# Fixed places for the weight tiles of column products, and later transposes, in a one-core decoder layer

## Chip, core and metric

The kernel runs on one core of a Trainium2 chip. The metric is the device time of one launch in microseconds. The kernel before takes 2506.86 us in the median of three runs (2506.35 to 2507.48). All times below are microseconds unless marked ns. The engines go by the names of the profile: PE (TensorE, matmuls), PEld (its weight loads), DVE (VectorE), ACT (ScalarE), POOL (GpSimd), SP (SyncE, which here issues the DMAs).

## What is computed

One hybrid decoder layer in float32 on 256 tokens with 2048 features:

```python
h = rmsnorm(x, ffn1_norm_pre)
x = x + 0.5 * rmsnorm((silu(h @ w_gate) * (h @ w_up)) @ w_down, ffn1_norm_post)   # D_FF = 5632
h = rmsnorm(x, mix_norm_pre)
c_q, c_kv, k_rope, hq, hf, hi, hg, gate_a, gate_b = split_columns(h @ w_in)       # 512, 512, 64, 6 x 2048
y_a = mla_branch(...)     # 16 heads; latents normed, up-projected, rotary part of 64, causal softmax
y_b = hgrn2_branch(...)   # 16 heads; gated linear recurrence over chunks
y = (sigmoid(gate_a) * y_a + sigmoid(gate_b) * y_b) @ w_out
x = x + rmsnorm(y, mix_norm_post)
h = rmsnorm(x, ffn2_norm_pre)
x = x + 0.5 * rmsnorm((silu(h @ w_gate) * (h @ w_up)) @ w_down, ffn2_norm_post)
```

All products are float32 in accuracy. The kernel gets it by splitting every operand into a rounded part `hi` (type fp32r) and the rest `lo`, and by computing hi x hi + hi x lo + lo x hi.

## The kernel before

Tokens are two tiles of 128 (`tt` = 0, 1). An operand of a product lies in one tile of 128 partitions x 2 x 16 x 256 floats: `hi` and `lo` of 16 slices (k) of 128 features by 256 tokens, features on the partitions. Such operands are h1, after1 and h2 (one tag, so one address), oa and ob (one tag), mg, and, with four slices, cqT and ckvT. The trace names the first three h, after and h.

**Weights.** `load_w` (L89) fetches 512 KB (128 x 1024 floats, tile `raw`, four buffers) by a DMA from SP's queue. ACT casts it to `whi` (L106) and DVE subtracts to get `wlo` (L107). `whi` and `wlo` come from `part` (L85): four buffers each of 1088 floats a partition, of which 1024 are used from an offset `place` on, counted in floats. `places` gives one offset for `whi` and one for `wlo`.

**Column products** (`gemm_t`, L116) give features by tokens: the weights are the stationary operand (loaded into PE before each matmul), the operand's slices are streamed. A weight group of 1024 columns serves 4 slices x 2 output blocks. For each of these 8 there is a pair: `wlo` over the 256 tokens of the operand's `hi` (L133) and `whi` over the 512 columns of `hi` and `lo` (L134). In the first slice of a product the two stand in the other order (L130, L131). A product has `kt / 4` groups: four for 16 slices, one for cqT and ckvT. `round` (L110) hands out the places, a new combination for each group in the order of the program: group i has `whi` at i % 8 * 8 and `wlo` at i // 8 % 8 * 8 floats, a multiple of 32 bytes each.

**Row products** (`gemm_n`, L153) give tokens by features: the operand's slices are stationary and `whi`, `wlo` are streamed, three matmuls a slice and token tile (L149 to L151). Both parts lie at `place`, which is SAME = 32 floats unless told otherwise. With `late`, the second token tile's matmuls are held back and run after the first tile's; `hooks` are pairs of a position and a function. The position is a fraction: from -1 to 0 over the first half, from 0 to 1 over the held half.

The program has 528 column groups. In their order: 160 in the first FFN, 48 in the MLA part (gates of after, and cqT and ckvT), 32 of oa, 76 in the HGRN2 part (after), 52 of ob and the last gates, 160 in the second FFN.

**End of a block.** `closing` (L271) runs four row products. The last one holds its second half back (16 slices). At position 0, `end` (L289) finishes the norm of token tile 0 and updates x; at HOOK = 0.7, `begin` (L299) builds the next operand of tile 0: `prenorm` (L257) does for four quarters of 512 features a broadcast load, a DVE product into `xn` (two buffers), four PE transposes (L249 in `transposed`) and the split on ACT and DVE (L190, L191). Tile 1 follows inside the next product (`w_cq` of the mixer, `gate0` of the second FFN) by a hook at NEXT = -0.1. DVE's products and the splits are pulled ahead in the planner by a priority of 400.

**MLA.** `latent` (L543) norms a 512-wide latent: ACT square sum, POOL power, DVE scaling into `xn` (L552), then PE transposes and the split. It runs for c_q, then, after the product with `w_ckv`, for c_kv. The rotary key product (L578 to L587) and `gate(0)` follow, then its rotation and two transposes (L600). `q_rope` (L607) makes the rotary queries: a product, DVE and POOL rotation into `xn`, PE transposes (L614). `heads_in` (L618) makes two heads' operands with column products of cqT and ckvT; between them `step` takes one deferred function from `later`.

PE runs its instructions in one order, which a planner (a list by priority and estimated readiness) fixes when the program is built. It starts from the program's order and may let ready work pass.

Of the kernel before, what the change touches and what calls it, by code (L numbers as in the profile page):

```python
# [9 lines left out]
F32 = mybir.dt.float32  # L10
# [4 lines left out]
ALU = mybir.AluOpType  # L15
# [4 lines left out]
P = 128  # L20
T = 256
NT = 2
D = 2048
KD = D // P
# [4 lines left out]
KL = LORA // P  # L29
NH = 16  # L30
ROPE = 64
# [6 lines left out]


AHEAD = 400  # L40
HOOK = 0.7
NEXT = -0.1


WARM = 10
# [1 line left out]
SAME = 32  # L47
# [17 lines left out]
class Ops:  # L65


    def __init__(self, ctx, tc, a):
        self.tc, self.nc, self.a = tc, tc.nc, a
        self.const = ctx.enter_context(tc.tile_pool(name="const", bufs=1))  # L70
        self.wp = ctx.enter_context(tc.tile_pool(name="wp", bufs=1))
        self.small = ctx.enter_context(tc.tile_pool(name="small", bufs=3))
        self.hp = ctx.enter_context(tc.tile_pool(name="hp", bufs=1))
        self.mm = ctx.enter_context(tc.tile_pool(name="mm", bufs=2, space=PSUM))
        self.tp = ctx.enter_context(tc.tile_pool(name="tp", bufs=2, space=PSUM))
        self.sp = ctx.enter_context(tc.tile_pool(name="sp", bufs=2, space=PSUM))
        self.dram = ctx.enter_context(tc.tile_pool(name="dram", bufs=1, space=DRAM))
        self.slots = KF // 4
        self.count = 0
        self.mhalf = self.const.tile([P, 8], F32, name="mhalf")  # L80
        self.nc.vector.memset(self.mhalf, -0.5)
        self.ident = self.const.tile([P, P], F32, name="ident")
# [24 lines left out]
        nc.vector.tensor_tensor(out=lo, in0=raw, in1=hi.bitcast(F32), op=ALU.subtract)  # L107
        return hi, lo

    def round(self):  # L110

        i = self.count
        self.count += 1
        return i % 8 * 8, i // 8 % 8 * 8

    def gemm_t(self, w, act, kt, tick=None):  # L116

        nc = self.nc  # L120
        ps = self.mm.tile([P, 2, 512], F32, name="mm")
        for g in range(kt // 4):
            hi, lo = self.load_w(w[g], places=self.round())
            for i in range(4):
                k = g * 4 + i
                for j in range(2):
                    c = slice(i * 256 + j * P, i * 256 + (j + 1) * P)
                    both = act(k)
                    if k == 0:
                        nc.tensor.matmul(ps[:, j], hi[:, c], both, start=True, stop=False)  # L130
                        nc.tensor.matmul(ps[:, j, 0:T], lo[:, c], both[:, 0], start=False, stop=False)  # L131
                    else:
                        nc.tensor.matmul(ps[:, j, 0:T], lo[:, c], both[:, 0], start=False, stop=False)  # L133
                        nc.tensor.matmul(ps[:, j], hi[:, c], both, start=False, stop=k == kt - 1)  # L134
            if tick:
                tick()
        return ps
# [116 lines left out]
    def ahead(self):  # L254
        return self.tc.high_priority(AHEAD)

    def prenorm(self, x, wname, act, tt):  # L257

        for c in range(4):
            with self.ahead():  # L260
                w = self.bcast(wname, c)
                xn = self.small.tile([P, 512], F32, name="xn", bufs=2)
                self.nc.vector.tensor_tensor(out=xn, in0=x[:, c * 512:(c + 1) * 512], in1=w, op=ALU.mult)  # L263
            self.transposed(xn, act, c, tt)

    def weighted(self, ps, c, z, wname):

# [3 lines left out]
    def closing(self, w, act, kt, late, own, pool, post, half, x_src, x_dst, nxt):  # L271

        z = [pool.tile([P, D], F32, name="z", tag=f"z{tt}") for tt in range(NT)]
        yssq = [self.ssq4() for _ in range(NT)]
        for c in range(3):
            ps = self.gemm_n(w[c], act, kt)
            for tt in range(NT):
                self.square_sum(yssq[tt][:, c:c + 1], ps[:, tt], D, half)  # L280
                self.weighted(ps[:, tt], c, z[tt], post)
        rest = [self.small.tile([P, 1], F32, name="rest", bufs=4) for _ in range(NT)]
        for tt in range(NT):
            self.known(rest[tt], yssq[tt][:, 0:3], half)
        x = [pool.tile([P, D], F32, name="x", tag="s8", bufs=self.slots) for tt in range(NT)]
        for tt in range(NT):
            self.nc.sync.dma_start(out=x[tt], in_=x_src[tt])

        def end(ps, tt):  # L289
            self.square_sum(yssq[tt][:, 3:4], ps[tt], D, half)  # L290
            rstd = self.rstd(yssq[tt][:, 3:4], rest[tt])
            self.weighted(ps[tt], 3, z[tt], post)
            for c in range(4):
                cs = slice(c * 512, (c + 1) * 512)
                self.nc.vector.scalar_tensor_tensor(out=x[tt][:, cs], in0=z[tt][:, cs], scalar=rstd, in1=x[tt][:, cs],  # L295
                                                    op0=ALU.mult, op1=ALU.add)
                self.nc.sync.dma_start(out=x_dst[tt, :, cs], in_=x[tt][:, cs])

        def begin(tt):  # L299
            if nxt is None:  # L300
                return
            wname, act, fac = nxt
            self.prenorm(x[tt], wname, act, tt)
            ssq = self.ssq4()
            for c in range(4):
                self.square_sum(ssq[:, c:c + 1], x[tt][:, c * 512:(c + 1) * 512], D)
            self.factor(fac, ssq, tt)

        ps = self.gemm_n(w[3], act, kt, late=late, pool=pool, own=own,
                         hooks=[(0, lambda ps: end(ps, 0)), (HOOK, lambda _: begin(0))])  # L310
        end(ps, 1)
        return [(NEXT, lambda _: begin(1))]


@with_exitstack
# [223 lines left out]
def mla(ops, mp, c_q, hm, h, fac, rows, oa, gate):  # L539
    nc, a, small, tp, sp, ident = ops.nc, ops.a, ops.small, ops.tp, ops.sp, ops.ident  # L540
    V, S, G = nc.vector, nc.scalar, nc.gpsimd

    def latent(ps, name, norm):  # L543
        w = ops.bcast(norm, 0)
        res = mp.tile([P, 2, KL, T], F32R, name=name)
        for tt in range(NT):
            ssq = small.tile([P, 1], F32, name="cssq")
            y = ps[tt] if isinstance(ps, list) else ps[:, tt]
# [1 line left out]
            rstd = ops.rstd(ssq, fac[:, tt, 1:2])  # L550
            cn = small.tile([P, LORA], F32, name="xn", bufs=2)
            V.scalar_tensor_tensor(out=cn, in0=y, scalar=rstd, in1=w, op0=ALU.mult, op1=ALU.mult)  # L552
            ops.transposed(cn, res, 0, tt)
        return lambda k: res[:, :, k, :]

    def rope(dst, src, tt, n):

# [12 lines left out]
    cos, sin = rope_tables(ops, mp)  # L570
    amask = mp.tile([P, 3, P], F32, name="amask")
    nc.sync.dma_start(out=amask, in_=a["amask"])
    cq = latent(c_q, "cqT", "mla_q_norm")
    ckv = latent(ops.gemm_n(a["w_ckv"][0], h, KD), "ckvT", "mla_kv_norm")

    hi, lo = ops.load_w(a["w_krope"][0], places=(0, 0))  # L578
    ps = ops.mm.tile([P, 2, 512], F32, name="mm")
    for k in range(KD):  # L580
        c = slice(k * ROPE, (k + 1) * ROPE)
        o = ps[0:ROPE, 0, 0:T]
        nc.tensor.matmul(o, hi[:, c], hm[:, 0, k, :], start=k == 0, stop=False)
        nc.tensor.matmul(o, hi[:, c], hm[:, 1, k, :], start=False, stop=False)
        nc.tensor.matmul(o, lo[:, c], hm[:, 0, k, :], start=False, stop=k == KD - 1)
    krt = mp.tile([ROPE, T], F32, name="krt")
    V.tensor_tensor(out=krt, in0=ps[0:ROPE, 0, 0:T], in1=rows[0:ROPE], op=ALU.mult)  # L587
    gate(0)
    kr = mp.tile([P, NT, 2, ROPE], F32, name="kr", tag="krt")
    pt = tp.tile([P, 4, P], F32, name="tp")  # L590
    for tt in range(NT):
# [3 lines left out]
        V.tensor_copy(out=kr[:, tt, 1], in_=kr[:, tt, 0])  # L595
    krT = mp.tile([P, 2, T], F32, name="krT")
    G.memset(krT, 0.0)
    pt = tp.tile([P, 4, P], F32, name="tp")
    for tt in range(NT):
        nc.tensor.transpose(out=pt[:, tt], in_=kr[:, tt].rearrange("p a b -> p (a b)"), identity=ident)  # L600
    for j in range(2):
        b = slice(j * ROPE, (j + 1) * ROPE)
        V.tensor_copy(out=krT[b, j], in_=pt[b, 0:2].rearrange("p a b -> p (a b)"))

    qrT = mp.tile([P, NH // 2, T], F32, name="qrT")

    def q_rope(c):  # L607
        ps = ops.gemm_n(a["w_q_rope"][c], cq, KL, place=SAME - 16)
        for tt in range(NT):
            qr = small.tile([P, 8, ROPE], F32, name="xn", bufs=2)  # L610
            rope(qr, ps[:, tt].rearrange("p (a b) -> p a b", b=ROPE), tt, 8)
            pt = tp.tile([P, 4, P], F32, name="tp")
            for i in range(4):
                nc.tensor.transpose(out=pt[:, i], in_=qr[:, 2 * i:2 * i + 2].rearrange("p a b -> p (a b)"),  # L614
                                    identity=ident)
            S.copy(out=qrT[:, 4 * c:4 * c + 4, tt * P:(tt + 1) * P], in_=pt)

    def heads_in(pair, step):  # L618
        qn = mp.tile([P, 2, T], F32, name="qn", bufs=3)
        ops.total(qn, ops.gemm_t(a["w_q_nope"][pair], cq, KL))  # L620
        step()
        kn = mp.tile([P, 2, T], F32, name="kn", bufs=3)
        ops.total(kn, ops.gemm_t(a["w_k_nope"][pair], ckv, KL))
        step()
        ps = ops.gemm_n(a["w_v"][pair], ckv, KL, n=256, place=0)
        v = mp.tile([P, NT, 256], F32, name="v", bufs=3)
# [52 lines left out]
    later = []  # L679
# [2 lines left out]
        if later:  # L682
            later.pop(0)()

    q_rope(0)
    nxt = heads_in(0, step)
    gate(1)
    q_rope(1)
    for pair in range(8):
        cur = nxt  # L690
        if pair < 7:
# [326 lines left out]
```

## Time and profile before

| what | value |
|---|---|
| median of 3 runs | 2506.86 us |
| profiled execution, own time | 2506.64 us |
| its span, first to last instruction | 2504.7 us |
| mean granted TensorE clock | 0.999 |
| weight bytes and the like read from HBM | 473.61 MB |
| L133 and L134 with h, after, oa, ob: matmuls | 7680 |
| L149 to L151 with at, after, mg: matmuls of `whi` and `wlo` | 3228 |

The page's first part gives each engine's busy time and share of the span, its second the granted clock and the DMA traffic in 40 slices, its fourth the chain of work that ended last. Further views group instructions, list waits, show instructions by time, or sum busy time over chosen stretches. A matmul's listed duration overlaps the next one's, so its cost is read from one start to the next in the timeline.

### The profile page before, as it was taken

Reading aid. Unit: us, or ns where it says so; the run is one execution under the profiler, and the core shown is the slowest. Engines: PE = TensorE matmul, PEld = TensorE weight load, DVE = VectorE, ACT = ScalarE, POOL = GpSimd, SP = SyncE. Lnnn points to the kernel's source line nnn. Section 1 sums busy time; section 2 is a strip of 40 time slices with the busy share of each in tenths; the row PEclk is TensorE's granted clock in tenths of the full one; section 3 lists DMA queues with packets and bytes.
Section 4 is the critical chain, followed back from the end, with each engine's and each line's share of the span. In section 5 each row is a group of like instructions: output and inputs, shape, how many; then the busy total and the mean of one; then the engine's idle time right before and its main releaser. Section 6 shows DMA issues by size and latency. Waiting matters only on the chain.

```text
span 2504.7 us, 33918 instructions
## 1 busy us (share of the span) xinstructions
PE 2486.5 (99%) x13306; PEld 2136.1 (85%) x13306; DVE 1544.9 (62%) x1845; ACT 1210.7 (48%) x1605; POOL 82.2 (3%) x108
## 2 busy tenths in 40 slices
PE   9999999999999999999999999999999999999998
PEld 7888888888887898888888888888788888888887
DVE  6656656554466666558778876665656666564444
ACT  6444444444454566444555554445544444444433
POOL 0000000000001100000000001120000000000000
PEclk9999999999999999999999999999999999999999
DMA  8555555566685444565555555567655555555665
GB/s 302 184 190 190 186 191 187 188 194 207 202 286 181 160 136 151 187 189 185 171 167 175 169 168 172 191 225 240 223 188 190 186 192 186 189 190 194 201 201 187
DMA packets 137680, 482.12 MB, mean 192 GB/s; under 512 B 15920, under 2 KB 16432, under 8 KB 136752
## 3 DMA queue, kind: packets, MB, share of 16 engines
q1 hardware_dynamic: 137520, 479.96, 58.8%
q8 instruction: 104, 1.70, 0.3%
q14 instruction: 56, 0.46, 0.1%
HBM read 473.61 MB, written 6.29 MB: 192 GB/s over the span
## 4 chain that ended last, share of the span: by engine, by line
PE 97%; DVE 1%; POOL 1%; DMA 1%; issue 1%; ACT 0%; SPq 0%; DVEq 0%; POOLq 0%; ACTq 0%
PE mm L134 36%; PE mm L133 18%; PE mm L151 12%; PE mm L150 11%; PE mm L149 11%; PE mm L130 3%; PE mm L131 1%; PE sp L852 1%; PE sp L640 0%; PE sp L639 0%; DVE x L295 0%; PE sp L840 0%; PE tp L671 0%; DVE xn L263 0%; DVE wlo L107 0%
## 5 line engine op out<-in xcount | busy, mean ns | idle before, releaser
L107 DVE TENSOR_TENSOR wlo<-raw,whi 128x1024 fp32r<-128x1024 f32 x832 | 1031.5, 1242 | 685.3 <-ACT whi L106 679.0
L106 ACT CAST whi<-raw 128x1024 fp32r<-128x1024 f32 x832 | 872.5, 1050 | 848.5 <-PE mm L134 452.7
L134 PE MATMUL mm<-h,whi 128*128 128x512 f32 x2400 | 842.2, 394 | 0.0
L133 PE MATMUL mm<-h,wlo 128*128 128x256 f32 x2400 | 672.0, 280 | 0.0
L134 PEld LDWEIGHTS mm<-h,whi 128*128 128x128 f32 x2400 | 450.9, 188 | 101.1
L133 PEld LDWEIGHTS mm<-h,wlo 128*128 128x128 f32 x2400 | 451.2, 188 | 3.5
L134 PE MATMUL mm<-after,whi 128*128 128x512 f32 x960 | 337.8, 394 | 0.0
L133 PE MATMUL mm<-after,wlo 128*128 128x256 f32 x960 | 270.6, 282 | 0.0
L149 PE MATMUL mm<-whi,at 128*128 128x512 f32 x664 | 258.3, 389 | 0.0
L150 PE MATMUL mm<-wlo,at 128*128 128x512 f32 x664 | 258.3, 389 | 0.0
L151 PE MATMUL mm<-whi,at 128*128 128x512 f32 x664 | 258.0, 389 | 0.0
L134 PEld LDWEIGHTS mm<-after,whi 128*128 128x128 f32 x960 | 180.4, 188 | 39.3
L133 PEld LDWEIGHTS mm<-after,wlo 128*128 128x128 f32 x960 | 180.6, 188 | 1.5
L150 PEld LDWEIGHTS mm<-wlo,at 128*128 128x128 f32 x664 | 124.6, 188 | 26.0
L149 PEld LDWEIGHTS mm<-whi,at 128*128 128x128 f32 x664 | 124.6, 188 | 25.9
L151 PEld LDWEIGHTS mm<-whi,at 128*128 128x128 f32 x664 | 124.6, 188 | 25.8
L149 PE MATMUL mm<-whi,after 128*128 128x512 f32 x304 | 121.6, 400 | 0.4 <-ACT after L190 0.4
L151 PE MATMUL mm<-whi,after 128*128 128x512 f32 x304 | 118.9, 391 | 0.0
L150 PE MATMUL mm<-wlo,after 128*128 128x512 f32 x304 | 118.5, 390 | 0.0
L134 PE MATMUL mm<-ob,whi 128*128 128x512 f32 x240 | 84.3, 394 | 0.0
L134 PE MATMUL mm<-oa,whi 128*128 128x512 f32 x240 | 84.1, 393 | 0.0
L141 ACT COPY m<-mm 128x512 f32<-128x512 f32 x56 | 32.8, 587 | 95.8 <-PE mm L134 95.8
(306 smaller groups left out, 2814.0 us busy)
## 6 DMA issues: line engine op xcount, KB each, us to landing
raw<-in_ffn_w_down SPq DMA_DIRECT2D x176, 512.0 KB, 4.3
raw<-in_ffn_w_gate SPq DMA_DIRECT2D x175, 512.0 KB, 4.3
raw<-in_ffn_w_up SPq DMA_DIRECT2D x175, 512.0 KB, 4.3
raw<-in_w_ga SPq DMA_DIRECT2D x32, 512.0 KB, 3.5
raw<-in_mla_w_o SPq DMA_DIRECT2D x32, 512.0 KB, 3.8
raw<-in_w_hq SPq DMA_DIRECT2D x32, 512.0 KB, 3.7
raw<-in_w_hf SPq DMA_DIRECT2D x32, 512.0 KB, 3.5
raw<-in_w_hi SPq DMA_DIRECT2D x32, 512.0 KB, 3.5
```

The source lines that it names most:

```text
L106: nc.scalar.copy(out=hi, in_=raw)
L107: nc.vector.tensor_tensor(out=lo, in0=raw, in1=hi.bitcast(F32), op=ALU.subtract)
L130: nc.tensor.matmul(ps[:, j], hi[:, c], both, start=True, stop=False)
L131: nc.tensor.matmul(ps[:, j, 0:T], lo[:, c], both[:, 0], start=False, stop=False)
L133: nc.tensor.matmul(ps[:, j, 0:T], lo[:, c], both[:, 0], start=False, stop=False)
L134: nc.tensor.matmul(ps[:, j], hi[:, c], both, start=False, stop=k == kt - 1)
L141: self.nc.scalar.copy(out=out, in_=ps[:, :, T:512])
L149: nc.tensor.matmul(o, both[:, 0, r], hi[:, c], start=k == 0, stop=False)
L150: nc.tensor.matmul(o, both[:, 0, r], lo[:, c], start=False, stop=False)
L151: nc.tensor.matmul(o, both[:, 1, r], hi[:, c], start=False, stop=k == kt - 1)
L852: nc.tensor.matmul(ps[:, 0, j], B[:, j], A[:, j], start=True, stop=True)
```

## The change

- `round` and its counter are gone. `gemm_t` takes a `place` (SAME by default) and puts `whi` at `place - 16` and `wlo` at `place`. The products with cqT and ckvT pass SAME - 16.
- `begin` does one quarter a call. Tile 0's quarters hang at 0.45, 0.45, 0.6 and 0.75 of the held half of the last product, tile 1's at -0.5, -0.5, -0.05 and 0.2 of the next one. The square sums and the factor come with the last quarter.
- `latent` scales both token tiles, then calls `between`, and only then transposes. For c_q, `between` is the product with `w_ckv`; for c_kv it is the rotary key product with `gate(0)`.
- `q_rope` returns its transposes as a function. `q_rope(0)`'s and the rotary key's second transposes go into `later`; `q_rope(1)`'s run after `gate(1)`.

```diff
-HOOK = 0.7
-NEXT = -0.1
+HOOK = (0.45, 0.45, 0.6, 0.75)
+NEXT = (-0.5, -0.5, -0.05, 0.2)
...
-    def round(self):
-
-        i = self.count
-        self.count += 1
-        return i % 8 * 8, i // 8 % 8 * 8
-
-    def gemm_t(self, w, act, kt, tick=None):
+    def gemm_t(self, w, act, kt, tick=None, place=SAME):
...
-            hi, lo = self.load_w(w[g], places=self.round())
+            hi, lo = self.load_w(w[g], places=(place - 16, place))
...
-    def prenorm(self, x, wname, act, tt):
-
-        for c in range(4):
-            with self.ahead():
-                w = self.bcast(wname, c)
-                xn = self.small.tile([P, 512], F32, name="xn", bufs=2)
-                self.nc.vector.tensor_tensor(out=xn, in0=x[:, c * 512:(c + 1) * 512], in1=w, op=ALU.mult)
-            self.transposed(xn, act, c, tt)
+    def prenorm(self, x, wname, act, tt, c):
+
+        with self.ahead():
+            w = self.bcast(wname, c)
+            xn = self.small.tile([P, 512], F32, name="xn", bufs=2)
+            self.nc.vector.tensor_tensor(out=xn, in0=x[:, c * 512:(c + 1) * 512], in1=w, op=ALU.mult)
+        self.transposed(xn, act, c, tt)
...
-        def begin(tt):
+        def begin(tt, c):
+
             if nxt is None:
                 return
             wname, act, fac = nxt
-            self.prenorm(x[tt], wname, act, tt)
-            ssq = self.ssq4()
-            for c in range(4):
-                self.square_sum(ssq[:, c:c + 1], x[tt][:, c * 512:(c + 1) * 512], D)
-            self.factor(fac, ssq, tt)
+            self.prenorm(x[tt], wname, act, tt, c)
+            if c == 3:
+                ssq = self.ssq4()
+                for i in range(4):
+                    self.square_sum(ssq[:, i:i + 1], x[tt][:, i * 512:(i + 1) * 512], D)
+                self.factor(fac, ssq, tt)
+
+        def parts(tt, places):
+            return [(at, lambda _, c=c: begin(tt, c)) for c, at in enumerate(places)]
 
         ps = self.gemm_n(w[3], act, kt, late=late, pool=pool, own=own,
-                         hooks=[(0, lambda ps: end(ps, 0)), (HOOK, lambda _: begin(0))])
+                         hooks=[(0, lambda ps: end(ps, 0)), *parts(0, HOOK)])
         end(ps, 1)
-        return [(NEXT, lambda _: begin(1))]
+        return parts(1, NEXT)
...
-    def latent(ps, name, norm):
+    def latent(ps, name, norm, between):
...
-            ops.transposed(cn, res, 0, tt)
-        return lambda k: res[:, :, k, :]
+            cns.append(cn)
+        got = between()
+        for tt in range(NT):
+            ops.transposed(cns[tt], res, 0, tt)
+        return lambda k: res[:, :, k, :], got
...
-    cq = latent(c_q, "cqT", "mla_q_norm")
-    ckv = latent(ops.gemm_n(a["w_ckv"][0], h, KD), "ckvT", "mla_kv_norm")
+    cq, c_kv = latent(c_q, "cqT", "mla_q_norm", lambda: ops.gemm_n(a["w_ckv"][0], h, KD))
...
+    ckv, krt = latent(c_kv, "ckvT", "mla_kv_norm", rope_product)
...
-    q_rope(0)
+    later += [q_rope(0), k_turned]
     nxt = heads_in(0, step)
+    turned = q_rope(1)
     gate(1)
-    q_rope(1)
+    turned()
```

`rope_product` holds the lines of the rotary key product and `gate(0)`, `k_turned` those of the key's second transposes; `turned` is `q_rope`'s loop of transposes and copies. Their instructions are the same as before.

More of the change, by code (lines that the diff above doesn't have):

```diff
@@ L78, in __init__ @@
         self.slots = KF // 4
-        self.count = 0
         self.mhalf = self.const.tile([P, 8], F32, name="mhalf")
@@ L541, in mla @@
     V, S, G = nc.vector, nc.scalar, nc.gpsimd
-    def latent(ps, name, norm):
+    def latent(ps, name, norm, between):
         w = ops.bcast(norm, 0)
         res = mp.tile([P, 2, KL, T], F32R, name=name)
+        cns = []
         for tt in range(NT):
@@ L572, in mla, with rope_product @@
     nc.sync.dma_start(out=amask, in_=a["amask"])
-    cq = latent(c_q, "cqT", "mla_q_norm")
-    ckv = latent(ops.gemm_n(a["w_ckv"][0], h, KD), "ckvT", "mla_kv_norm")
[L578 to L588, printed above, removed]
+    cq, c_kv = latent(c_q, "cqT", "mla_q_norm", lambda: ops.gemm_n(a["w_ckv"][0], h, KD))
+    def rope_product():
+        hi, lo = ops.load_w(a["w_krope"][0], places=(0, 0))
+        ps = ops.mm.tile([P, 2, 512], F32, name="mm")
+        for k in range(KD):
+            c = slice(k * ROPE, (k + 1) * ROPE)
+            o = ps[0:ROPE, 0, 0:T]
+            nc.tensor.matmul(o, hi[:, c], hm[:, 0, k, :], start=k == 0, stop=False)
+            nc.tensor.matmul(o, hi[:, c], hm[:, 1, k, :], start=False, stop=False)
+            nc.tensor.matmul(o, lo[:, c], hm[:, 0, k, :], start=False, stop=k == KD - 1)
+        krt = mp.tile([ROPE, T], F32, name="krt")
+        V.tensor_tensor(out=krt, in0=ps[0:ROPE, 0, 0:T], in1=rows[0:ROPE], op=ALU.mult)
+        gate(0)
+        return krt
+    ckv, krt = latent(c_kv, "ckvT", "mla_kv_norm", rope_product)
     kr = mp.tile([P, NT, 2, ROPE], F32, name="kr", tag="krt")
@@ L597, in mla, with k_turned @@
     G.memset(krT, 0.0)
[L598 to L603, printed above, removed]
+    def k_turned():
+        pt = tp.tile([P, 4, P], F32, name="tp")
+        for tt in range(NT):
+            nc.tensor.transpose(out=pt[:, tt], in_=kr[:, tt].rearrange("p a b -> p (a b)"), identity=ident)
+        for j in range(2):
+            b = slice(j * ROPE, (j + 1) * ROPE)
+            V.tensor_copy(out=krT[b, j], in_=pt[b, 0:2].rearrange("p a b -> p (a b)"))
     qrT = mp.tile([P, NH // 2, T], F32, name="qrT")
@@ L608, in q_rope @@
         ps = ops.gemm_n(a["w_q_rope"][c], cq, KL, place=SAME - 16)
+        qrs = []
         for tt in range(NT):
@@ L611, in q_rope, with turned @@
             rope(qr, ps[:, tt].rearrange("p (a b) -> p a b", b=ROPE), tt, 8)
[L612 to L616, printed above, removed]
+            qrs.append(qr)
+        def turned():
+            for tt in range(NT):
+                pt = tp.tile([P, 4, P], F32, name="tp")
+                for i in range(4):
+                    nc.tensor.transpose(out=pt[:, i], in_=qrs[tt][:, 2 * i:2 * i + 2].rearrange("p a b -> p (a b)"),
+                                        identity=ident)
+                S.copy(out=qrT[:, 4 * c:4 * c + 4, tt * P:(tt + 1) * P], in_=pt)
+        return turned
     def heads_in(pair, step):
         qn = mp.tile([P, 2, T], F32, name="qn", bufs=3)
-        ops.total(qn, ops.gemm_t(a["w_q_nope"][pair], cq, KL))
+        ops.total(qn, ops.gemm_t(a["w_q_nope"][pair], cq, KL, place=SAME - 16))
         step()
         kn = mp.tile([P, 2, T], F32, name="kn", bufs=3)
-        ops.total(kn, ops.gemm_t(a["w_k_nope"][pair], ckv, KL))
+        ops.total(kn, ops.gemm_t(a["w_k_nope"][pair], ckv, KL, place=SAME - 16))
         step()
```

## The prediction

> **What bounds the kernel now.** I read the page first: its busy shares, the granted clock and the chain of work that ended last.
>
> ```profile
> PE 2486.5 (99%) x13306; PEld 2136.1 (85%) x13306; DVE 1544.9 (62%) x1845; ACT 1210.7 (48%) x1605; POOL 82.2 (3%) x108
> PEclk9999999999999999999999999999999999999999
> GB/s 302 184 190 190 186 191 187 188 194 207 202 286 181 160 136 151 187 189 185 171 167 175 169 168 172 191 225 240 223 188 190 186 192 186 189 190 194 201 201 187
> PE 97%; DVE 1%; POOL 1%; DMA 1%; issue 1%; ACT 0%; SPq 0%; DVEq 0%; POOLq 0%; ACTq 0%
> ```
>
> TensorE (PE) is busy 99% of the span at a full granted clock and is 97% of the chain. So the time is the sum of the intervals from one matmul's start to the next, plus a few stalls, and there are two ways to gain: shorter intervals, or fewer stalls. Busy time can't show the first, because matmuls overlap (in rows further down, one listed with 0.39 us is followed 0.23 us later). So I went on to the stretches in which PE does column products (`gemm_t`) and almost nothing else. The first number is the length, the x after PE the matmuls.
>
> ```profile
> 63.41:499.72 436.31, 436.31 (x2499) 381.89 (x2498) 265.47 (x274) 206.60 (x235) 0.00 (x0) 1.00 0.58 188
> 1009.46:1098.87 89.41, 89.41 (x515) 78.39 (x514) 53.38 (x49) 40.24 (x44) 9.03 (x7) 1.00 0.62 192
> 1526.03:1671.37 145.34, 145.34 (x833) 127.26 (x832) 87.27 (x78) 67.61 (x78) 24.11 (x14) 1.00 0.57 187
> 1809.72:2257.17 447.45, 447.45 (x2563) 391.62 (x2561) 269.43 (x277) 210.10 (x239) 0.00 (x0) 1.00 0.58 188
> ```
>
> By the loops these hold 156, 32, 52 and 160 weight groups; a group is one `load_w` and 8 pairs of a 256-column `wlo` and a 512-column `whi` matmul. Together 400 groups take 1118.51 us: 2.796 us a group, 349.5 ns a pair. The few matmuls over 16 a group are neighbours at the edges. PE never idles there (busy equals length).
>
> **Part 1: fixed places.** Before, `round()` gives group number i of the program the places (i % 8 * 8, i // 8 % 8 * 8) floats for `whi` and `wlo`: all 64 combinations pass in turn. Afterwards every group whose operand is h, after, oa or ob has (16, 32); with cqT and ckvT it is (0, 16), as those tiles lie 64 bytes lower modulo 256 in the program's allocation. The old kernel visits that very combination eight times: groups 34, 98, 162, 226, 290, 354, 418 and 482. The kernel before is thus its own experiment. Group 34 is the third group of the ninth column product of the first FFN (products start with an L130 matmul, the ninth with the first row below). Its rows in the timeline of PE (first column the start), then its neighbour 38, which has (48, 32), then the starts of groups 98 (again h, 64 groups on), 226 (oa) and 418 (second FFN) and of the groups behind them:
>
> ```profile
> 141.92 0.39 PE L130 MATMUL mm<-h,whi 128*128 128x512 f32 x1
> ...
> 144.74 0.28 PE L133 MATMUL mm<-h,wlo 128*128 128x256 f32 x1
> ...
> 147.53 0.28 PE L133 MATMUL mm<-h,wlo 128*128 128x256 f32 x1
> 147.64 0.39 PE L134 MATMUL mm<-h,whi 128*128 128x512 f32 x1
> 147.87 0.28 PE L133 MATMUL mm<-h,wlo 128*128 128x256 f32 x1
> ...
> 150.25 0.28 PE L133 MATMUL mm<-h,wlo 128*128 128x256 f32 x1
> ...
> 158.61 0.28 PE L133 MATMUL mm<-h,wlo 128*128 128x256 f32 x1
> ...
> 161.44 0.28 PE L133 MATMUL mm<-h,wlo 128*128 128x256 f32 x1
> ```
>
> ```profile
> 326.43 0.28 PE L133 MATMUL mm<-h,wlo 128*128 128x256 f32 x1
> ...
> 329.15 0.28 PE L133 MATMUL mm<-h,wlo 128*128 128x256 f32 x1
> 1059.89 0.28 PE L133 MATMUL mm<-oa,wlo 128*128 128x256 f32 x1
> ...
> 1062.61 0.28 PE L133 MATMUL mm<-oa,wlo 128*128 128x256 f32 x1
> 1949.72 0.28 PE L133 MATMUL mm<-h,wlo 128*128 128x256 f32 x1
> ...
> 1952.44 0.28 PE L133 MATMUL mm<-h,wlo 128*128 128x256 f32 x1
> ```
>
> Group 33, at (8, 32), takes 147.53 - 144.74 = 2.79 us; group 34 takes 2.72, 340 ns a pair, and so do the three others shown (the four not shown differ by 3 ns at most); group 38 takes 2.83, 353 ns a pair. Nothing but places and buffers differs between these groups. That 2.72 comes back with another operand and 1800 us later says that the place decides, not the moment. The tile of 1088 floats is 4352 = 17 x 256 bytes long, so all four buffers keep the same place modulo 256 bytes.
>
> Sum: 1118.51 - 400 x 2.72 = 30.5 us for the four stretches. I take 30: the first two pairs of each product run in another order (`whi` first), and a steady pattern may take a pair or two to set in.
>
> The other 128 groups (48 in MLA, 76 in HGRN2, 4 ahead of the first stretch) would give 128 x 0.076 = 9.8 us at most. Two stretches hold nearly all of them:
>
> ```profile
> 800.23:1009.45 209.22, 207.87 (x1270) 184.47 (x1269) 135.20 (x239) 121.56 (x201) 10.43 (x15) 1.00 0.46 149
> 1098.88:1526.02 427.14, 427.14 (x2337) 369.06 (x2336) 330.62 (x481) 229.19 (x386) 18.29 (x30) 1.00 0.53 173
> ```
>
> There short matmuls of heads or scan stand between the groups and the pattern starts anew each time. No row shows how fast (16, 32) recovers from a break, so I bound it by 0 and 9.8 and take 60%: 6 us.
>
> Cover: a shorter group needs its 512 KB of weights in 2.72 us, 193 GB/s where the stretches now move 188; the page's slices reach 302. Splitting a group takes DVE 1.24 and ACT 1.05 us of its 2.72:
>
> ```profile
> L107 DVE TENSOR_TENSOR wlo<-raw,whi 128x1024 fp32r<-128x1024 f32 x832 | 1031.5, 1242 | 685.3 <-ACT whi L106 679.0
> L106 ACT CAST whi<-raw 128x1024 fp32r<-128x1024 f32 x832 | 872.5, 1050 | 848.5 <-PE mm L134 452.7
> ```
>
> ACT's idle time ends on PE (a free buffer), so supply runs ahead. If that cover were gone, PE would wait for `whi`.
>
> By the Trainium skill, page SBUF — State Buffer, section "Who interferes with whom", PE has two independent read ports, one for the moving operand and one for weight loads, and never waits on anyone. By that rule places could not matter and this part would give 0. The trace disagrees: 2.72 against 2.83 us with nothing else changed.
>
> **Part 2: transposes behind the next products, quarters apart.** Here stalls go. These are PE's waits in the view of waits (total us, times, longest), without those of the kernel's start:
>
> ```profile
> PE tp L249 <- DVE xn L552: 2.6, 3, 1.0
> PE tp L614 <- POOL xn L568: 1.4, 4, 0.7
> PE mm L149 <- ACT h L190: 0.9, 1, 0.9
> PE tp L249 <- DVE after L191: 0.8, 2, 0.5
> PE mm L150 <- DVE wpair L107: 0.8, 2, 0.6
> PE tp L249 <- DVE h L191: 0.5, 1, 0.5
> PE mm L149 <- ACT after L190: 0.4, 1, 0.4
> ```
>
> The latents' transposes (L552) wait for a chain of ACT square, POOL power and DVE scaling while ready products stand behind them. Moved behind the `w_ckv` product and behind the rope product with `gate(0)`, they have many microseconds of cover: 2.6 us go. What is late next is `heads_in(0)`, which needs ckvT: four short splitting instructions, under the `w_q_rope` product. Of the rotary queries' 1.4 us, those of `q_rope(1)`, with the longest of 0.7, go behind `gate(1)`: say 0.8; those of `q_rope(0)` I leave, since only one product of four k steps, as now, lies ahead of them. No instruction is added, DMAs and SP's broadcasts included. Part: -3.4.
>
> For the quarters, the second half of `w_down`'s last product starts at 728.25 and has 16 steps of three matmuls, 0.68 us each:
>
> ```profile
> 728.25 0.39 PE L149 MATMUL mm<-whi,at 128*128 128x512 f32 x1
> 731.53 1.28 DVE L263 TENSOR_TENSOR xn<-x,wbc 128x512 f32<-128x512 f32 x2
> 736.41 1.03 PE L249 MATMUL tp<-ident,xn 128*128 128x128 f32 x8
> ```
>
> At 0.7 the first eight transposes come at step 12, 736.41. At 0.45 they come at step 8, 733.7, and their two `xn` are done at 732.81: no new wait. The third quarter needs an `xn` buffer that these transposes free, then a DVE slot; at step 10 it has 1.4 us for a 0.68 us product in DVE's queue, with `wlo` of 1.24 us competing. If one gets ahead, PE stalls about a microsecond, and the steps queued behind it wait too. For the operand's second half, the quarters at -0.5, -0.5, -0.05 and 0.2 split the burst on which the rows with after, h and `wpair` (3.4 us) hang. Bounds: +2 (a stall of a microsecond at each of two places) to -3.4; I take half the gain, -1.7.
>
> **Sum.** -30 - 6 - 3.4 - 1.7 = -41.1 us. The profiled execution took 2506.64 us (span 2504.7 and 1.9 around it), 0.2 below the median of the runs shown: 2506.86 - 41.1 = 2465.8 us.
>
> **Rivals.**
>
> *Slower: the fixed place settles in a bad pattern.* A pair's time isn't set by the places alone. Group 294 has (48, 32) like group 38; behind a break it runs at 340 ns: seven pairs between these two rows.
>
> ```profile
> 1407.18 0.28 PE L133 MATMUL mm<-after,wlo 128*128 128x256 f32 x1
> ...
> 1409.56 0.28 PE L133 MATMUL mm<-after,wlo 128*128 128x256 f32 x1
> ```
>
> So one place can hold two steady patterns, 340 and 353 ns, and how it is entered chooses. (16, 32) was always entered from (8, 32). If a product's first pairs threw it into a pattern of 353 ns, all 528 groups would cost 2.83: 528 x 0.034 = +18, with the stalls' -5.1: 2520 us. It turns slower than before once nearly four fifths of the groups run so (0.034 lost on each of those against 0.076 won on each other one, and 5.1 of stalls). Against it: all eight visits were at 340, from the first pair on. Chance 0.07.
>
> *The good pattern is lost at every product's start and comes back halfway:* half of 30.5 + 9.8, -20 - 5 = 2482 us. Chance 0.12.
>
> *The places give nothing:* what made group 34 fast was its turn in the sequence and not its place. Stalls alone: 2502 us. The equal rows under h, oa and the second FFN's h speak against it; the rule of SBUF — State Buffer in the Trainium skill quoted above would give this time. Chance 0.06.
>
> *The forecast:* 0.75.
>
> **How the numbers follow.** Everything at its best (40.3 and all 7.4 of stalls) gives 2459, and waits are shorter than the delays from start to start, so the low end is 2456. The high end reaches past the halfway case, to 2488; this leaves out the last rivals and a margin for the first, under 2 in 10. A measurement here can tell about 0.2% (5 us) from no change: below 2501.8 is faster. Faster: 0.75 + 0.12 + half of 0.06 = 0.90; same 0.03; slower 0.07.
>
> **What would show it.** Groups of column products in the FFN stretches starting 2.72 us apart, with 113 and 227 ns between starts, and stretches of 160 groups near 435 us instead of 447; none of PE's waits on L552 left, and fewer on L190 and L191. Wrong: groups at 2.79 or 2.83, PE waiting for `whi` or `raw`, or new waits of L249 on `xn`.

## The result and the profile after

The changed kernel takes 2467.71 us in the median of four runs (2466.83 to 2467.96), beside 2506.70 (2506.35 to 2507.48) for the kernel before: a ratio of 0.9843, 95% interval 0.9826 to 0.986. The prediction was 2465.8 us in a range of 2456 to 2488. The slowest run of the changed kernel lies 38.4 us below the fastest of the kernel before. The profiled execution took 2467.53 us, with a span of 2465.7.

From the page of the changed kernel, its busy shares, the granted clock and the shares by engine of the chain that ended last:

```profile
PE 2452.0 (99%) x13306; PEld 2119.1 (86%) x13306; DVE 1544.4 (63%) x1845; ACT 1211.6 (49%) x1605; POOL 83.3 (3%) x108
PEclk9999999999999999999999999999999999999999
PE 29%; DVE 1%; issue 0%; POOL 0%; ACT 0%; DVEq 0%; POOLq 0%; ACTq 0%
```

The instruction counts are those of before, the clock is full and PE is busy for the same 99%: a share of busy time can't show such a gain. The chain was followed back over only about 30% of the span this time, and PE is nearly all of that part. In the view of windows, the four stretches of column products (first, third, fifth and sixth row) and the two of MLA and HGRN2 (second and fourth); the first number behind the bounds is the length:

```profile
63.79:489.54 425.75, 425.75 (x2500) 376.48 (x2498) 265.51 (x274) 207.53 (x236) 0.00 (x0) 1.00 0.59 193
785.13:990.99 205.86, 205.56 (x1278) 184.35 (x1277) 136.42 (x241) 122.18 (x203) 10.06 (x15) 1.00 0.48 155
990.99:1078.63 87.64, 87.64 (x515) 77.38 (x514) 53.43 (x49) 40.28 (x44) 9.07 (x7) 1.00 0.61 194
1078.63:1501.28 422.65, 422.65 (x2337) 366.75 (x2336) 330.65 (x481) 229.41 (x386) 18.32 (x30) 1.00 0.54 175
1501.28:1643.07 141.79, 141.79 (x833) 125.39 (x832) 87.24 (x78) 67.65 (x78) 24.05 (x14) 1.00 0.59 191
1781.59:2218.23 436.64, 436.64 (x2563) 386.09 (x2562) 269.47 (x277) 211.13 (x239) 0.00 (x0) 1.00 0.59 192
```

The four stretches with nothing but column products lost 10.56, 1.77, 3.55 and 10.81 us against the lengths of before: 26.7 us for 400 groups. PE still never idles in them (busy equals length), and the weights come at 191 to 194 GB/s where they came at 187 to 192. So the work got shorter with the same instructions.

The first matmuls of the first six column groups in PE's timeline (first column the start):

```profile
52.10 0.40 PE L123 MATMUL mm<-h,whi 128*128 128x512 f32 x1
...
54.85 0.28 PE L126 MATMUL mm<-h,wlo 128*128 128x256 f32 x1
...
57.57 0.28 PE L126 MATMUL mm<-h,wlo 128*128 128x256 f32 x1
...
60.29 0.28 PE L126 MATMUL mm<-h,wlo 128*128 128x256 f32 x1
...
63.80 0.48 PE L123 MATMUL mm<-h,whi 128*128 128x512 f32 x1
...
66.68 0.28 PE L126 MATMUL mm<-h,wlo 128*128 128x256 f32 x1
...
69.48 0.28 PE L126 MATMUL mm<-h,wlo 128*128 128x256 f32 x1
```

Three things are to be read here. Groups inside a product take 2.72 us (54.85 to 57.57 to 60.29). The first group of a product takes 2.75 (52.10 to 54.85). And the second product, entered behind transposes at 63.80, runs its groups at 2.80, 350 ns a pair (66.68 to 69.48), with the same places. By the starts, 156 of the 160 groups of each FFN have 340 ns pairs and these four, or four like them, 350.

PE's waits without those of the kernel's start (total us, times, longest):

```profile
PE mm L142 <- ACT h L183: 1.2, 1, 1.2
...
PE mm L143 <- DVE wpair L106: 0.7, 1, 0.7
...
PE tp L242 <- DVE h L184: 0.4, 1, 0.4
PE tp L242 <- DVE after L184: 0.3, 1, 0.3
PE tp L627 <- POOL xn L570: 0.2, 1, 0.2
```

The 2.6 us on the latents' `xn` are gone, and of the 1.4 us on the rotary `xn` 0.2 are left. At the two handovers between blocks, waits on `h`, `after` and `wpair` remain, with one of 1.2 us that is longer than any there before.

### The profile page after: what moved, and what is told of

Read it like the earlier page. It is cut to its first block, busy times and chain, and to the rows that moved or that the text cites. A ratio compares the mean times of both kernels' runs of the same rounds, so it can differ in the third digit from the quotient of the medians.

```text
span 2465.7 us, 33906 instructions
## 1 busy us (share of the span) xinstructions
PE 2452.0 (99%) x13306; PEld 2119.1 (86%) x13306; DVE 1544.4 (63%) x1845; ACT 1211.6 (49%) x1605; POOL 83.3 (3%) x108
## 5 line engine op out<-in xcount | busy, mean ns | idle before, releaser
L127 PE MATMUL mm<-h,whi 128*128 128x512 f32 x2400 | 820.8, 389 | 0.0
L126 PE MATMUL mm<-h,wlo 128*128 128x256 f32 x2400 | 663.3, 276 | 0.0
L127 PE MATMUL mm<-after,whi 128*128 128x512 f32 x960 | 330.1, 390 | 0.0
```

## The experiments

Times are medians. In all jobs the kernel before took 2506.55 to 2506.90 us. The changed kernel was measured in the job of the result alone, so differences from it of a microsecond or two are read across jobs.

### Places alone, and moves alone

The kernel before with nothing but the fixed places (the products with cqT and ckvT again 16 floats lower), and the changed kernel with the old `round`:

```diff
# first: the kernel before
-            hi, lo = self.load_w(w[g], places=self.round())
+            hi, lo = self.load_w(w[g], places=(place - 16, place))
# second: the changed kernel
-            hi, lo = self.load_w(w[g], places=(place - 16, place))
+            hi, lo = self.load_w(w[g], places=self.round())
```

> The kernel before with the fixed places alone, nothing moved. Theory (the place sets the pair time): pairs of 340 ns in nearly all of the 528 groups, 2506.7 - 36 = 2471 us. Rival (the new order of the work did it, the places nothing): the gain of the stalls is gone, so about 2506 us, pairs still at 349.5 ns on average.

Measured: 2473.11 us (2472.95 to 2473.58, four runs), ratio 0.9867 (0.9851 to 0.9882), -33.6 us. The first FFN's stretch is 425.75 us long, as in the changed kernel, and PE's waits are those of before:

```profile
PE tp L249 <- DVE xn L552: 2.6, 3, 1.0
PE tp L614 <- POOL xn L568: 1.5, 4, 0.7
```

> The changed kernel with the old changing places: only the moves are left. Theory: pairs at 349.5 ns on average; the moved latents and rotary transposes save about 3.4 us and the quarters nearly nothing, 2503 us. Rival (places give nothing): about 2468 us, as the whole change.

Measured: 2500.98 us (2500.73 to 2501.93), ratio 0.9978 (0.9969 to 0.9986), -5.7 us. The two parts add up to -39.3, and the whole change gave -39.0: to within 0.4 us they simply add.

### The quarters together again

```diff
-HOOK = (0.45, 0.45, 0.6, 0.75)
-NEXT = (-0.5, -0.5, -0.05, 0.2)
+HOOK = (0.7, 0.7, 0.7, 0.7)
+NEXT = (-0.1, -0.1, -0.1, -0.1)
```

> The changed kernel with the quarters at their old positions (0.7 four times, -0.1 four times). If the quarters apart gave 1.7 us as forecast: 2469.4 us. If they gave nothing, since the handover hangs on the chain of norm, x, transposes and ACT's casts and not on the hook: within 1 us of the changed kernel's 2467.7 us.

Measured: 2467.60 us (2467.23 to 2467.63), ratio 0.9844 (0.983 to 0.9857): the same as the changed kernel. Setting the quarters apart is worth nothing, and the whole 5.7 us belong to the transposes of MLA.

### The rotary transposes back

`q_rope` transposes at once again, and `k_turned` runs ahead of `q_rope(0)`; the latents' transposes stay moved.

```diff
-    later += [q_rope(0), k_turned]
+    k_turned()
+    q_rope(0)
...
-    turned = q_rope(1)
     gate(1)
-    turned()
+    q_rope(1)
```

> The changed kernel, but the transposes of the rotary queries and of the rotary key stand where they stood before (each right behind its rotation, the key's ahead of q_rope(0), q_rope(1) behind gate(1)); the latents' transposes stay moved. The moves give 5.7 us together by the earlier runs. Theory from the starts of the matmuls: the latents are most of it, at least 4 us, and this run gives 2468.5 to 2469.5 us with PE's waits of L249-type transposes on the rotary xn back at 0.8 to 1.4 us. Rival by the view of waits alone (2.6 us for the latents): 2470.5 to 2471.

Measured: 2470.50 us (2469.53 to 2471.29), ratio 0.9855 (0.9842 to 0.9869). So the rotary part is worth about 2.8 us and the latents, by difference, the other 2.9; the theory that the latents are most of it fell. This run's waits, then one of them in PE's timeline (the bracket gives the idle time before a row and what ended it):

```profile
PE tp L627 <- POOL xn L570: 1.9, 3, 1.0
```

```profile
807.28 0.28 PE L124 MATMUL mm<-ckvT,wlo 128*128 128x256 f32 x1
808.55 0.66 PE L627 MATMUL tp<-ident,xn 128*128 128x128 f32 x4 [0.99 <-POOL xn L570]
```

The wait is listed with 0.99 us, but from the start of the 256-column matmul to the transposes 1.27 us pass, where such a matmul is followed after 0.11 to 0.12 in the rows above: the stall costs 1.15.

### Other fixed places

`whi` 64 bytes above the operand instead of 64 below, and `whi` 64 above with `wlo` 64 below:

```diff
-            hi, lo = self.load_w(w[g], places=(place - 16, place))
+            hi, lo = self.load_w(w[g], places=(place + 16, place))        # first
+            hi, lo = self.load_w(w[g], places=(place + 16, place - 16))   # second
```

> The changed kernel with whi 64 bytes behind wlo's place in the other direction, (48, 32), the place that showed both 353 and 340 ns in the kernel before. If the place alone set the time (353 seen in seven of eight visits): 2467.7 + 528 x 0.105 = 2523 us. If the way of entry decides and a product's start acts like the break ahead of group 294: pairs of 340 ns, about 2468 us. A mixture by product lies between.

Measured: 2501.56 us (one run). All 160 groups of the first FFN have pairs of 350 ns, two starts of groups being 2.80 us apart:

```profile
65.88 0.28 PE L126 MATMUL mm<-h,wlo 128*128 128x256 f32 x1
...
68.68 0.28 PE L126 MATMUL mm<-h,wlo 128*128 128x256 f32 x1
```

In HGRN2's 76 groups the same places give 350 ns in 59, 353 or 354 in 9 and 340 in 8. One place has several steady patterns. Which one follows an opening (the start of a product) hangs on the place: the first product of oa runs at 340 ns here, behind transposes, and from the next opening on all 28 groups run at 350; in the changed kernel the first one runs at 350 and the openings bring 340. (In the kernel before, six of the eight visits to this place were at 353 ns, not seven: group 166 settled at 349 to 351.)

> The changed kernel with whi at place + 16 and wlo at place - 16 floats: (48, 16) with h, after, oa and ob, (32, 0) with cqT and ckvT. In the kernel before all eight groups at (48, 16) took 2.83 us, 353 ns a pair. Theory that the place decides: groups of 2.83 in nearly all of the 528, 528 x 0.11 = +58 us less what product starts change: 2515 to 2526 us, slower than the kernel before. Rival that the sequence decides, or that any fixed place settles well: about 2468.

Measured: 2514.65 us (one run), above the kernel before. The second FFN's stretch is 451.0 us long, where it was 447.45 before and 436.64 in the changed kernel:

```profile
1814.32:2265.34 451.02, 451.02 (x2563) 394.64 (x2562) 269.48 (x277) 210.28 (x239) 0.00 (x0) 1.00 0.58 186
```

Here 120 of its 160 groups run at 353 or 354 ns; the other 40, the first of each product, are at 350 and slide back to 353 without a break. (Of the eight visits in the kernel before seven took 2.83 us; the eighth, behind a break, 2.88.) It is the places and not the constancy that the change lives on: a fixed place can be worse than the mix.

### The order within a pair

`whi` first in every slice, so that the two kinds alternate across products too; and the same with the last slice the other way round.

```diff
-                    if k == 0:
+                    if True:            # first run; second run: if k < kt - 1
-                        nc.tensor.matmul(ps[:, j], hi[:, c], both, start=True, stop=False)
-                        nc.tensor.matmul(ps[:, j, 0:T], lo[:, c], both[:, 0], start=False, stop=False)
+                        nc.tensor.matmul(ps[:, j], hi[:, c], both, start=k == 0, stop=False)
+                        nc.tensor.matmul(ps[:, j, 0:T], lo[:, c], both[:, 0], start=False, stop=k == kt - 1)
```

> The changed kernel, but in every slice of a column product whi comes first and wlo second, so that the two alternate without a break through a product and from one product into the next. In the changed kernel the first slice's pairs are whi, wlo and all others wlo, whi: two whi matmuls stand next to each other at every product's start (the last of the product before and the first of the new one), and two wlo matmuls where slice 0 goes into slice 1. Theory: the first group of a product takes 2.747 us instead of 2.720 because of those two places; without them all groups take 2.720, 132 products x 0.027 = -3.6 us, about 2464.0 against 2467.7. Rival: the 27 ns belong to the start of a product in itself (a new result tile, slice 0 again), whatever the order: 2467.7. If whi first settles in another steady pattern (350 ns a pair), some 528 x 0.08 = +42 us: 2510.

> As the run before, but the last slice of each product has wlo first and whi last: the two neighbours of one kind (two wlo where slice 14 goes into slice 15, two whi between products) stand at the end and at the border. Theory that neighbours of one kind cost the time: as the changed kernel, 2467.7 us. Rival that it is only the order of the first slices: near 2464.

Measured: 2468.12 (2466.99 to 2469.33) and 2468.55 us (2468.28 to 2469.01), both the same as the changed kernel within what can be told. Under the first total lies a gain that is given back. The third column product of the first FFN in the timelines of the changed kernel and of this run, its first group's start and the next group's:

```profile
75.08 0.40 PE L123 MATMUL mm<-h,whi 128*128 128x512 f32 x1
...
77.83 0.28 PE L126 MATMUL mm<-h,wlo 128*128 128x256 f32 x1
```

```profile
74.95 0.39 PE L123 MATMUL mm<-h,whi 128*128 128x512 f32 x1
...
77.67 0.39 PE L123 MATMUL mm<-h,whi 128*128 128x512 f32 x1
```

2.75 us became 2.72: the opening of a product costs nothing once no two matmuls of one kind stand side by side. All 400 groups of the four stretches are now at 340 ns, also those that ran at 350. But MLA's stretch grew from 205.86 to 209.72 us, and PE has new waits there:

```profile
783.40:993.12 209.72, 207.05 (x1278) 184.43 (x1277) 136.01 (x241) 122.53 (x203) 10.99 (x15) 1.00 0.48 153
```

```profile
PE tp L683 <- ACT pT L676: 1.3, 3, 0.4
PE tp L624 <- POOL xn L567: 1.2, 1, 1.2
```

With a `wlo` matmul last, `whi` is free one matmul before the product's end, and the planner puts the next group's cast on ACT ahead of the copy of the result; `pT` queues behind. The second run shows that it is the neighbours of one kind that cost: with them moved to the end of the product, the first FFN's groups sum up to the changed kernel's value again (436.65 us, against 435.33 with strict alternation). The starts of the second FFN show the place in both kernels: the second `whi` in a row is followed after 236 ns instead of 227, the second `wlo` after 122 instead of 113.

So the next run keeps the old order in MLA (gates and heads); 112 products have the new one:

```diff
+                    if first:
+                        nc.tensor.matmul(ps[:, j], hi[:, c], both, start=k == 0, stop=False)
+                        nc.tensor.matmul(ps[:, j, 0:T], lo[:, c], both[:, 0], start=False, stop=k == kt - 1)
-                    if k == 0:
+                    elif k == 0:
...
-            pg = ops.gemm_t(wg[c], act, KD)
+            pg = ops.gemm_t(wg[c], act, KD, first=True)   # so also wu, mla_w_o, hgrn_w_o, w_hq, w_hf
```

> whi first in every slice only for the products of 16 slices with h, oa and ob and the two of HGRN2 (114 products); the gates and the heads' products of the MLA part keep the changed kernel's order. In the run with whi first everywhere the FFN, oa, HGRN2 and ob groups together lost 3.9 us, and the MLA groups gained 3.1, with PE waiting on the rotary queries' xn (1.2) and on pT (1.3), because ACT now casts the next group ahead of copying a product's result. Theory: the opening cost is gone and the MLA part is as in the changed kernel, 2467.7 - 3.8 = 2463.9 us. Rival: the time comes back elsewhere (ACT's later copies hold up result tiles): 2466 to 2468.

Measured: 2466.18 us (2465.97 to 2466.37), ratio 0.9836 (0.9823 to 0.985), -1.5 us against the changed kernel. MLA is as in the changed kernel. What came back came elsewhere than the rival said: the stretch of oa is 2.0 us longer,

```profile
989.01:1078.69 89.68, 89.68 (x515) 78.47 (x514) 47.84 (x49) 40.25 (x44) 9.12 (x7) 1.00 0.58 192
```

with all 32 groups at 350 ns, and the first eight of HGRN2 behind them as well, up to the next break. Without neighbours of one kind nothing disturbed this pattern, though a bad one: entered wrongly, it held for 40 groups, where the changed kernel's openings bring 28 of oa's 32 back to 340. HGRN2's groups cost 0.4 us more than in the changed kernel, where strict alternation everywhere had saved 0.4.

### The square sums behind the casts

Why did the quarters give nothing? At the handover to the second FFN, PE and ACT in the timelines of the changed kernel:

```profile
1737.99 1.03 PE L242 MATMUL tp<-ident,xn 128*128 128x128 f32 x8
1740.23 0.50 PE L142 MATMUL mm<-whi,h 128*128 128x512 f32 x1 [1.21 <-ACT h L183]
```

```profile
1738.23 0.63 ACT L190 ACTIVATE junk<-x 128x512 bf16<-128x512 f32 x1 [1.05 <-DVE x L287]
...
1738.99 0.63 ACT L190 ACTIVATE junk<-x 128x512 bf16<-128x512 f32 x1
...
1739.62 1.05 ACT L183 CAST h<-tp 128x512 fp32r<-128x512 f32 x2
```

PE waits for the cast of the first transposes, and ACT does two square sums of the next norm first. The cast starts 1.63 us after the transposes do. The planner pulls the sums ahead as soon as x is there, wherever their hook stands: in the run with the quarters together ACT again does two of them (at 1737.68 and 1738.43) before the cast (1739.06), 1.33 us behind the start of the transposes, and PE waits 0.9 us on `h`. So the sums of token tile 1 were made to wait, by a bias of zeros computed from the operand's second quarter:

```diff
+                zero = None
+                if tt:
+                    zero = self.small.tile([P, 1], F32, name="zero", bufs=2)
+                    self.nc.vector.tensor_scalar(out=zero, in0=act[:, 1, 7, T - 1:T].bitcast(F32), scalar1=0.0,
+                                                 scalar2=None, op0=ALU.mult)
...
-                    self.square_sum(ssq[:, i:i + 1], x[tt][:, i * 512:(i + 1) * 512], D)
+                    self.square_sum(ssq[:, i:i + 1], x[tt][:, i * 512:(i + 1) * 512], D, bias=zero)
```

> The changed kernel, but the four square sums of token tile 1 at each handover wait for the second quarter of the operand (their bias is a column of zeros made from it), so that ACT does the operand's casts first; one DVE product of 128 values is added per handover. Theory: the quarters gave nothing because ACT takes two square sums of 0.8 us between x and the first casts, and PE's wait for the first half of the operand hangs on that; with the casts first the wait on ACT's h of 1.2 us is gone and some of the wait in the mixer's handover: -1 to -2.3 us, 2465.4 to 2466.7. Rival: the chain from the last product over the norm to x sets the handover, or wpair is late next: 2467.5 or more.

> The two edits of this call together. If they are independent, 2467.7 - 3.8 - 1.5: about 2462.4 us, below both kernels; if either rival holds, 2464 to 2467.

Measured: 2511.59 us (2510.34 to 2513.43, 11 runs), ratio 1.0019 (1.001 to 1.0028), and for both edits 2518.40 (2509.72 to 2519.42), ratio 1.0046 (1.0032 to 1.006). The theories of both runs missed by over 40 us, and not through the sums: the wait on `h` did fall from 1.2 to 0.2 us. The row products of `w_down` in the timelines of this run and of the changed kernel, three matmuls from row to row:

```profile
600.13 0.39 PE L142 MATMUL mm<-whi,at 128*128 128x512 f32 x1
...
600.83 0.39 PE L142 MATMUL mm<-whi,at 128*128 128x512 f32 x1
```

```profile
599.70 0.39 PE L142 MATMUL mm<-whi,at 128*128 128x512 f32 x1
...
600.38 0.39 PE L142 MATMUL mm<-whi,at 128*128 128x512 f32 x1
```

A step takes 0.70 us instead of 0.68, in a part of the code that wasn't touched; column pairs take 346 to 347 ns. In the program's allocation the new tile, two buffers of 4 bytes a partition laid 32 bytes apart, pushed the operands h1, after1, h2, at, oa, ob, cqT and ckvT up by 64 bytes. Relative to the operand, modulo 256, `whi` now lies at -128 and `wlo` at -64 in a column product; in row products both weights lie at -64 where they lay at 0. The tile mg stayed where it was, and its matmuls still follow each other in 227 ns. The `wpair` tiles, which hold part of the weights of the held halves, moved up with the operands: with at, after and h their matmuls still take 227 ns, but with mg, which stayed and so lies 64 bytes below them (modulo 256), 231. So it is the distance between weights and operand that counts, and not either address alone. By the sum over starts the column groups cost 24.4 us more, the row products with at 13.2, with after 4.1 and with h 1.4: 43.1 of the 45.3 us between the two profiled executions. The run with both edits took 2509.72 us once and 2518.31 to 2519.42 four times; only the first of these was profiled, so what the others lost stays open.

The last run, against the one with both edits, takes the zeros from a tile that was there, and keeps `whi` first to the FFNs and ob:

```diff
-                    zero = self.small.tile([P, 1], F32, name="zero", bufs=2)
+                    zero = self.ssq4()[:, 0:1]
...
-            py = ops.gemm_t(a["mla_w_o"][c], lambda k: oa[:, :, k, :], KD, first=True)
+            py = ops.gemm_t(a["mla_w_o"][c], lambda k: oa[:, :, k, :], KD)   # so also w_hq, w_hf
```

> The run with the square sums' wait took 2511.6 us because its column of zeros, a new tile of 8 bytes, moved every operand behind it up by 64 bytes: whi then lay 128 and wlo 64 bytes below the operand (modulo 256), pairs took 346.6 ns and row products 233.5 ns a matmul instead of 226.7. Here the zeros lie in a tile that was there already (one more of the sums' own), and the operands lie as in the changed kernel. whi comes first in every slice of the FFNs' and ob's products alone, as oa's 32 groups all ran at 350 ns with whi first. Theory: pairs of 340 and row products of 226.7 ns are back; the FFN and ob groups lose 2.9 us, the sums another 1 to 2 by PE's wait on ACT's h of 1.2 us: 2462.8 to 2463.8. Rival 1, the sums give nothing: 2464.9. Rival 2, it was the sums' wait and not the address that cost 44 us: over 2500.

Measured: 2464.77 us (2463.58 to 2465.20, five runs), ratio 0.9831 (0.9818 to 0.9845): the fastest median of all, and all five runs lie below those of the changed kernel. It settles the address: the sums' wait is in it, and the 44 us are gone. For the sums the first rival holds. In ACT's and PE's timelines of this run:

```profile
1737.45 1.07 ACT L186 CAST h<-tp 128x512 fp32r<-128x512 f32 x2 [5.13 <-PE tp L246]
```

```profile
1738.09 0.50 PE L145 MATMUL mm<-whi,h 128*128 128x512 f32 x1 [0.24 <-ACT h L186]
...
1746.33 0.50 PE L146 MATMUL mm<-wpair,h 128*128 128x512 f32 x1 [0.36 <-DVE wpair L106]
...
1767.17 0.50 PE L146 MATMUL mm<-wpair,h 128*128 128x512 f32 x1 [0.21 <-DVE wpair L106]
```

ACT casts 0.63 us after the start of the transposes (1736.82), and the wait of 1.21 us is 0.24. But PE, a microsecond earlier, now meets `wpair` twice: the splitting of the weights is late next, and takes the time back: by the sum over starts, everything outside the column products takes 1007.9 us in both kernels. The gain of 2.9 us is that of the order in the FFNs and ob (first FFN 436.65 to 435.33 us, second 436.64 to 435.38, ob 141.79 to 141.59: 2.8).

## Why the prediction was right, step by step

**PE's intervals bound the kernel, and places set them: right.** Five layouts of weights and operand, with nearly the same instructions and the same clock, gave 2467.7, 2501.6, 2511.6, 2514.7 and (all 64 in turn, with the moves) 2501.0 us. By the rule of the Trainium skill (page SBUF — State Buffer, section "Who interferes with whom") that PE never waits on anyone, places would have given 0; the 33.6 us measured for places alone speak against that reading. Whether it is PE's reads that get in each other's way no run here shows.

**The four stretches, -30: measured -26.7.** The 3.8 us short of 30.5 are two terms that the prediction put at 0.5 together: the openings cost 0.027 us for each of some 97 products (2.6), and 12 groups run at 350 ns, 0.08 each (1.0). Both were gone with strict alternation, where the four stretches lost another 3.5 us.

**The other 128 groups, -6: measured -6.9** (33.6 of places alone less 26.7). The 60% were a little low; HGRN2's groups are nearly all at 340 (75 of 76), so the pattern comes back within a few pairs of a break, and what is lost there lies in those pairs. In MLA, with places alone, 10 of the 48 groups stayed at 350.

**Latents and rotary queries, -3.4: measured -5.7.** The mechanism was right, the size was read from the wrong view. For the latents 2.6 was close (2.9). For the rotary queries 0.8 was far off (2.8). There the prediction left `q_rope(0)`'s stalls in, saying that only one product lay ahead of them; as deferred functions its transposes are hidden too. And a wait in the list of waits is shorter than the delay from start to start, as the rows of 0.99 and 1.15 us show; the prediction named that and used it for the low end alone.

**Quarters, -1.7: measured 0.** The step that failed is that the stalls hang on where the transposes stand. They hang on ACT, which does two square sums ahead of the casts, and behind that on the split of `wpair`. The bounds of +2 and -3.4 held the value, but half the gain was a guess between them.

**The rivals.** The slower one is a real mechanism: the run with (48, 16) took 2514.7 us, beside the 2520 it was priced at. It did not strike at (16, 32), except in the few groups at 350 ns. The opposite of the second rival was true: here a product's opening does not lose the good pattern but brings it back. What the prediction's eight visits couldn't show is that these places have a 350 ns pattern too: they were always entered from the same neighbour.

The errors nearly cancel: +2.4 for the places, -2.3 for the moves, +1.7 for the quarters, 1.8 us in the sum, against 1.9 from forecast to result.

## What to carry to other kernels

Where PE is busy all the time, measure start to start, group by group: if equal groups differ with nothing but their addresses, the kernel holds its own experiment, and the addresses of weights and operand are worth a look before any rearrangement: here they gave 33.6 us, all the moved transposes 5.7. Such a gain hangs on the allocation: any new tile ahead of the operands can move it, so look at the addresses and at one untouched product after every edit. Before moving work to remove a wait, see what the awaited engine does in that time; and read a stall's worth from starts, not from the list of waits.

## What was not expected of the hardware

- A pair of a 256- and a 512-column matmul has several steady patterns at one and the same place: 340 and 350 ns with `whi` at -64 and `wlo` at 0 bytes from the operand (modulo 256), 350, 353 and 340 at +64 and 0. At these two places nearly every change of pattern stood behind a break or at neighbours of one kind; without them 350 ns held for 40 groups, some 110 us, and 340 for the 156 of an FFN's stretch.
- At +64 and -64 it is mostly 353 ns, and 350 slides back to it; at -128 and -64 it is 346 to 347.
- Row products feel it as well: 227 ns a matmul of 512 columns with the streamed weights at the operand's own place, 233 with them 64 bytes below, 231 with them 64 bytes above. 340 ns a pair and 227 ns for 512 columns are the same 0.443 ns a column, and no layout tried went below that. Why these distances matter stays open.
